# RG-LRU steps paced one by one behind the chunks of a two-layer hybrid block, with state sums in PSUM

## The chip, the cores and the metric

The kernel runs on one core of a Trainium2 chip. The metric is the device time of one execution in microseconds (us). The time before is the median of three runs.

The engines are named as in the profile: PE (TensorE, matmuls; PEld is its weight load), DVE (VectorE), ACT (ScalarE), POOL (GpSimd) and SP (the queue that issues most DMAs). SBUF is the on-chip memory, PSUM the memory that matmuls write.

## The reference, cut to what matters

Two layers, each over 512 tokens of width 1024. One input projection feeds three branches, and their gated outputs go through one output projection.

```python
for l in range(DEPTH):
    xn = rms_norm(h, ln_g[l])
    proj = xn @ w_in[l]
    u_a, z_a, u_b, z_b, q_lat, kv_lat, k_rope, z_c = jnp.split(proj, pts, axis=-1)
    y_a = rwkv7_mix(u_a, ...)           # a recurrence over tokens, 8 heads of 64x64 state
    y_b = rms_norm(rglru_mix(u_b, ...), lru_out_g[l])
    y_c = rms_norm(mla_mix(q_lat, kv_lat, k_rope, ...), mla_out_g[l])
    y = concatenate([y_a * silu(z_a), y_b * silu(z_b), y_c * silu(z_c)])
    h = h + y @ w_out[l]
return rms_norm(h, final_g)

def rglru_mix(u, ...):                  # the RG-LRU branch
    xc = conv_b + sum(up[:, j:j + T] * conv_w[j] for j in range(4))
    gate_r = sigmoid(xb @ ga_w + ga_b); gate_i = sigmoid(xb @ gx_w + gx_b)
    log_a = -8 * gate_r * softplus(-lam)
    a = exp(log_a)
    bx = sqrt(-expm1(2 * log_a)) * (gate_i * xc)
    h = scan over tokens of  h = a * h + bx
```

## The kernel before, in words

Tokens lie along the columns, channels on the 128 partitions. A projection (`proj`) is 24 matmuls of 512 columns: 8 slices of the input, each with three products (lines 233 to 235), since every float32 operand is split into a rounded high part H and the remainder L. For a weight tile, `weights` loads the raw tile `wr`, rounds it on ACT to `wH`, and subtracts on POOL or DVE to `wL` (line 229); a counter with the modulus `wmod` sends every `wmod`-th of these subtractions to DVE. The high and low parts of activations are made by `ysplit` (ACT, then line 211 on DVE).

The RWKV recurrence is done in 8 chunks of 64 tokens, one after the other (`chunk`, step `H`). Chunk `ch` corrects its values from the state (PE line 849, then two additions on DVE, line 852), makes its contribution to the state (PE line 859), adds the old state (DVE line 863) and multiplies by the decay (DVE line 864; chunk 0 has only line 866) into a new state tile `S`. Every second chunk also makes the outputs of two chunks (PE lines 877 and 883, copied by DVE line 885 and squared by ACT line 886, reduced by DVE line 887). So the chunks are a serial chain that goes PE, DVE, PE, DVE, DVE, PE. Other work has to fill the engines meanwhile.

That other work is, in this stage: the RG-LRU branch's four tiles of 128 channels. `lru_a(j)` (step `A`) projects tile `j`, does the convolution (three DVE operations, line 681), makes two gates on PE (line 687) with their sigmoids, the product of gate and input (POOL line 691) and a tanh. `lru_b` (step `B`, two tiles per call) makes the decay and the factor: exp on ACT, a square on POOL (line 702), two DVE operations (704 and 705), a square root on ACT, a product on POOL (710), then the scan on DVE (712), its square for the norm (ACT lines 716 and 718, POOL line 719) and the gated product on DVE (720). Then there are the group norm of the recurrence (`N`), the latent products of the attention branch (`t`, 8 slices of 12 matmuls with 416 columns), the gates of that branch (`g`, one projection each), its latent statistics (`T1`) and the sums over tokens of the RG-LRU's squares (`R`, PE line 379).

The order in which this is written is the string `ORD3`, one letter and a number per step. A scheduler then places the instructions on each engine's queue, by the order of writing and by its own estimate of when inputs are ready. Each queue runs strictly in order. `act` chains those ACT operations that need a function table, and loads a table when the set changes.

Of the kernel before, what the change touches and what calls it, by code (L numbers as in the profile page):

```python
# [11 lines left out]
AF = mybir.ActivationFunctionType  # L12
# [35 lines left out]
def body(ctx, tc, x, wc, wl, wo, w2a2, gagx, wuq, wukv, vec, ln_g, fin_g, cst, out, depth=DEPTH):  # L48
# [17 lines left out]
    WA, WB, WC, WD = 1000, 2, 2, 5  # L66
# [5 lines left out]
    def g2(shape=(128, 512)):  # L72
        return tl("g2", shape, F32, bufs=11)
# [132 lines left out]
    def f(ap):  # L206
        return ap.bitcast(F32)
# [113 lines left out]
    def one_layer(l):  # L321
# [350 lines left out]
        def lru_a(*js, o=None):  # L672
            for j in js:
                o = o or proj(17 + j)
                ub = g2([128, T + 3])
                G.memset(ub[:, 0:3], 0.0)
                copy(ub[:, 3:], o)
                xc = g2()
                A.activation(out=xc, in_=o, func=AF.Identity, scale=vc("cw", 12 + j), bias=vc("cb", j))
                for t in range(3):  # L680
                    V.scalar_tensor_tensor(out=xc, in0=ub[:, t:t + T], scalar=vc("cw", 4 * t + j), in1=xc, op0=ALU.mult, op1=ALU.add)  # L681
                gt = []
                for w in range(2):
                    o = ps()
                    for e in range(2):
                        hr = slice(64 * e, 64 * e + 64)
                        PE.matmul(o[hr, :], gw[hr, w, j, :], xc[hr, :], start=True, stop=True)  # L687
                    s = g2()
                    act(s, o, AF.Sigmoid, bias=vc("gx_b" if w else "ga_b", j))
                    gt.append(s)  # L690
                G.tensor_tensor(out=gt[1], in0=gt[1], in1=xc, op=ALU.mult)
                th = g2()
                act(th, gt[0], AF.Tanh, scale=sp8[:, l, j:j + 1])
                st[j] = (gt[0], gt[1], th)
                o = None

        def lru_b(*js):
            for j in js:
                a, bx, th = st[j]
                act(a, a, AF.Exp, scale=nsp8[:, l, j:j + 1])  # L700
                a2 = g2()
                G.tensor_tensor(out=a2, in0=a, in1=a, op=ALU.mult)

                V.scalar_tensor_tensor(out=a2, in0=a2, scalar=1.0, in1=th, op0=ALU.add, op1=ALU.mult)
                V.tensor_scalar(out=a2, in0=a2, scalar1=1.0e-34, scalar2=None, op0=ALU.max)  # L705
                st[j] += (a2,)
            for j in js:
                a, bx, th, a2 = st[j]
                act(a2, a2, AF.Sqrt)
                G.tensor_tensor(out=bx, in0=bx, in1=a2, op=ALU.mult)  # L710
                hs = th
                V.tensor_tensor_scan(out=hs, data0=a, data1=bx, initial=0.0, op0=ALU.mult, op1=ALU.add)
                sq = a2
                if j == 0:
                    stb[0] = tl("sqn", [128, T])
                    A.activation(out=stb[0], in_=hs, func=AF.Square)
                else:
                    A.activation(out=sq, in_=hs, func=AF.Square)
                    G.tensor_tensor(out=stb[0], in0=stb[0], in1=sq, op=ALU.add)
                V.scalar_tensor_tensor(out=hs, in0=hs, scalar=vc("out_g", j), in1=gz[j], op0=ALU.mult, op1=ALU.mult)  # L720
                yb.append(hs)

# [118 lines left out]
        def chunk(ch):  # L841
            cp, par = ch // 2, ch % 2
            ur = slice(64 * (1 - par), 64 * (1 - par) + 64)
            if ch:
                uo = [ck([128, 4, 64]) for _ in range(2)]
                for p in range(4):
                    for e in range(2):
                        hr = slice(64 * e, 64 * e + 64)
                        PE.matmul(uo[e][ur, p, :], AR[p][hr, 0, ch * 64:(ch + 1) * 64], S[ch][hr, p, :], start=True, stop=True)
                for e in range(2):  # L850
                    u = UV[ur, :, ch, 64 * e:64 * e + 64]
                    V.tensor_tensor(out=u, in0=uo[e][ur, :, :], in1=u, op=ALU.add)
            if ch < 7:
                so = ck([128, 4, 64])
                for p in range(4):
                    for e in range(2):
                        hr = slice(64 * e, 64 * e + 64)
                        hc = slice(e * 64, (e + 1) * 64)
                        PE.matmul(so[hr, p, :], BT[p][:, ch, hc], UV[:, p, ch, hc], start=True, stop=True)
                sn = S[ch + 1] = tl("S", [128, 4, 64], bufs=3)  # L860
                pc = PC[:, :, ch:ch + 1].to_broadcast([128, 4, 64])
                if ch:
                    V.tensor_tensor(out=sn, in0=so, in1=S[ch], op=ALU.add)
                    V.tensor_tensor(out=sn, in0=sn, in1=pc, op=ALU.mult)
                else:
                    V.tensor_tensor(out=sn, in0=so, in1=pc, op=ALU.mult)
# [34 lines left out]
        def lat_products(kk):  # L901
            wmod[0] = WC
# [42 lines left out]
        steps.update({"H": chunk, "N": lambda _: group_norm(), "A": lru_a, "B": lambda i: lru_b(2 * i, 2 * i + 1), "R": b_sums, "Y": b_split,  # L945
# [280 lines left out]
```

## Time and profile before

| what | value |
|---|---|
| median of 3 runs | 852.93 us (851.06 to 854.30) |
| the profiled execution's own time | 854.13 us |
| its span, first to last instruction | 852.3 us |
| mean granted clock of PE | 0.986 |
| PE busy | 793.0 us, 93% |
| DVE, ACT, POOL busy | 561.1, 518.6, 326.3 us |
| ACT table loads | 31, of 1283 ns each in the mean |
| DMA | 91.07 MB, mean 107 GB/s |

The profile has one page of sums over the whole execution, and views of the trace that can be cut to a window. In a timeline row the columns are start, duration, engine, line, operation, output<-inputs, the shape, the count, and in brackets the idle time ahead of it with what ended it. In a row of waits they are the total, how many, and the longest. Line numbers of the profile are those of the kernel before; the changed kernel's lines are some 5 to 31 higher.

### The profile page before, as it was taken

What the parts mean: (1) busy time and instruction counts of PE and PEld (TensorE: products, weight loads), DVE (VectorE), ACT (ScalarE), POOL (GpSimd) and SP (SyncE); (2) the same over time, 40 slices, a digit from 0 to 9 for tenths busy, and PEclk for the clock granted to TensorE, in tenths of its full rate; (3) what the DMA queues carried; (4) which work ended last, traced back from release to release, by engine and by line L of the source; (5) the groups of instructions that cost most, each with busy time, mean ns of one, the idle gap of its engine ahead of it and who ended that gap; (6) DMA issues with size and microseconds to landing.
All of it is one profiled execution on the core that took longest, in us unless ns stands there. A gap on an engine that the chain in (4) does not pass through costs nothing.

```text
span 852.3 us, 15212 instructions
## 1 busy us (share of the span) xinstructions
PE 793.0 (93%) x5696; PEld 619.7 (73%) x5696; DVE 561.1 (66%) x1145; ACT 518.6 (61%) x1018; POOL 326.3 (38%) x299
## 2 busy tenths in 40 slices
PE   3999999999879999999979999999997899899995
PEld 3878888886659867656778788888765697675674
DVE  5578776924976486774474976695367955677636
ACT  5667876557563666564367677845566436665634
POOL 0455557522462332012344556574143524210223
PEclk9999999999998999999999999999999899999998
DMA  7322233311113365123733233232001235631354
GB/s 235 106 75 65 72 112 128 114 59 31 32 48 103 131 215 185 52 86 101 266 116 99 75 99 99 100 111 94 27 26 42 81 100 156 235 102 50 111 173 161
DMA packets 49754, 91.07 MB, mean 107 GB/s; under 512 B 5520, under 2 KB 8336, under 8 KB 49680
## 3 DMA queue, kind: packets, MB, share of 16 engines
q1 hardware_dynamic: 49104, 89.05, 32.5%
q8 instruction: 45, 0.74, 0.4%
q10 hardware_dynamic: 576, 1.05, 0.3%
q14 instruction: 29, 0.24, 0.1%
HBM read 73.30 MB, written 16.78 MB: 106 GB/s over the span
## 4 chain that ended last, share of the span: by engine, by line
PE 65%; DVE 15%; ACT 10%; DMA 4%; issue 3%; POOL 3%; SPq 0%; ACTq 0%; DVEq 0%; POOLq 0%
PE acc L233 15%; PE acc L234 14%; PE acc L235 14%; PE acc L1058 4%; PE ck L1084 3%; ACT g L138 3%; PE ps L1076 2%; ACT wH L141 1%; ACT UV L141 1%; PE ps L687 1%; DMA hp<-dr 1%; DVE g L681 1%; PE ps L611 1%; ACT L136 1%; PE ps L629 1%
## 5 line engine op out<-in xcount | busy, mean ns | idle before, releaser
L229 POOL TENSOR_TENSOR wL<-wr,wH 128x512 fp32r<-128x512 f32 (+1 forms) x126 | 170.4, 1355 | 298.2 <-ACT wH L141 270.7
L141 ACT ACTIVATE wH<-wr 128x512 fp32r<-128x512 f32 (+1 forms) x192 | 118.7, 621 | 139.9 <-PE acc L234 74.5
L233 PE MATMUL acc<-xH,wH 128*128 128x512 f32 (+1 forms) x496 | 192.6, 389 | 0.0
L234 PE MATMUL acc<-xL,wH 128*128 128x512 f32 (+1 forms) x496 | 189.8, 383 | 0.4 <-DVE xL L306 0.2
L235 PE MATMUL acc<-xH,wL 128*128 128x512 f32 (+1 forms) x496 | 189.1, 382 | 0.0
L233 PEld LDWEIGHTS acc<-xH,wH 128*128 128x128 f32 x496 | 94.4, 191 | 18.2 <-ACT xH L141 0.7
L235 PEld LDWEIGHTS acc<-xH,wL 128*128 128x128 f32 x496 | 94.5, 190 | 17.2
L234 PEld LDWEIGHTS acc<-xL,wH 128*128 128x128 f32 x496 | 94.5, 190 | 16.9 <-DVE xL L306 0.9
L229 DVE TENSOR_TENSOR wL<-wr,wH 128x512 fp32r<-128x512 f32 (+1 forms) x66 | 50.9, 774 | 72.2 <-ACT wH L141 72.2
L233 PE MATMUL acc<-wH,c 128*128 128x512 f32 x192 | 81.9, 427 | 1.4 <-DVE hp L428 1.1
L234 PE MATMUL acc<-wL,c 128*128 128x512 f32 x192 | 76.3, 397 | 0.0
L235 PE MATMUL acc<-wH,c 128*128 128x512 f32 x192 | 76.1, 397 | 0.0
L141 ACT ACTIVATE UV<-ps 64x512 f32<-64x512 f32 (+4 forms) x112 | 52.3, 494 | 30.5 <-PE ps L1076 22.4
L233 PEld LDWEIGHTS acc<-wH,c 128*128 128x128 f32 x192 | 36.1, 188 | 12.0 <-DVE hp L428 2.0
L138 ACT ACTIVATE c<-acc,sm 128x128 f32<-128x128 f32 (+3 forms) x64 | 33.6, 526 | 18.3 <-DVE sm L1060 18.1
L1058 PE MATMUL acc<-am,am 128*128 128x128 f32 (+3 forms) x128 | 42.3, 447 | 0.9 <-ACT c L138 0.8
L234 PEld LDWEIGHTS acc<-wL,c 128*128 128x128 f32 x192 | 36.2, 189 | 8.4 <-issue 1.4
L235 PEld LDWEIGHTS acc<-wH,c 128*128 128x128 f32 x192 | 36.1, 188 | 8.2 <-issue 0.5
L369 POOL TENSOR_TENSOR g<-g,g 128x512 f32<-128x512 f32 x24 | 32.2, 1340 | 24.1 <-ACT g L138 24.1
L136 ACT ACT_TABLE_LOAD x31 | 39.8, 1283 | 1.3 <-PEq L1214 0.7
L138 ACT ACTIVATE g<-g 128x512 f32<-128x512 f32 (+1 forms) x58 | 36.4, 628 | 4.6 <-DVE g L705 2.6
L141 ACT ACTIVATE c<-g 128x512 fp32r<-128x512 f32 (+1 forms) x40 | 24.9, 628 | 17.0 <-DVE g L720 7.0
(219 smaller groups left out, 1590.8 us busy)
## 6 DMA issues: line engine op xcount, KB each, us to landing
wr<-in_wc_dram SPq DMA_DIRECT2D x116, 256.0 KB, 2.6
wr<-in_wo_dram SPq DMA_DIRECT2D x48, 256.0 KB, 3.4
hp<-dr SPq DMA_DIRECT2D x38, 256.0 KB, 3.5
dr<-hp SPq DMA_DIRECT2D x28, 256.0 KB, 2.9
dr<-g SPq DMA_DIRECT2D x16, 256.0 KB, 2.6
g<-dr SPq DMA_DIRECT2D x16, 256.0 KB, 3.4
wr<-in_wl_dram SPq DMA_DIRECT2D x16, 208.0 KB, 2.5
dr<-c SPq DMA_DIRECT2D x12, 256.0 KB, 3.8
```

The lines of the kernel that those rows point to most:

```text
L136: chained(A.preload_act_table_set(SETS[st]))
L138: chained(A.activation(out=out, in_=in_, func=func, **kw))
L141: i = A.activation(out=out, in_=in_, func=AF.Copy, **kw)
L229: (V if wn[0] % wmod[0] == 0 or wn[0] <= 4 else G).tensor_tensor(out=L, in0=raw, in1=f(H), op=ALU.subtract)
L233: PE.matmul(o, a[0], b[0], start=start, stop=False)
L234: PE.matmul(o, a[0], b[1], start=False, stop=False)
L235: PE.matmul(o, a[1], b[0], start=False, stop=stop)
L369: G.tensor_tensor(out=z, in0=z, in1=s, op=ALU.mult)
L611: PE.matmul(os[e][:, cp, :].rearrange("p (x s) -> p x s", x=2), bk[rr, ch, :, :].rearrange("p x s -> p (x s)"), ar[rr, :, ch * 64:(ch + 1) ...
L1058: PE.matmul(o[:, 0:n], qT[:, hd, qt * 128:n], K2[:, p, e, 0:n], start=True, stop=True)
L1076: PE.transpose(o[:, (qt - kt) * 128:(qt - kt + 1) * 128], Pm[p][e, qt][:, kt * 128:(kt + 1) * 128], ident)
L1084: i = PE.matmul(ot[e * 64:(e + 1) * 64, k2 * 128:T], Vt[:, k2, 2 * p + e, :], PT[:, 2 * (k2 % 2) + e, 0:(4 - k2) * 128], start=(k2 == 0), ...
```

## The change

The change does five things, the same in both layers.

1. The RG-LRU steps are cut into single operations. `conv_steps(j)` projects tile `j` and gives back its three convolution operations as a list; `lru_b_steps` gives back, for each tile, a factor, a scan and a gated product. `A` and the new step `b` put them on the list `paced`. At two places of each chunk, behind the second correction and behind the state product, `pace` takes the next one from the list and issues it behind that DVE instruction (`tc.issue_after`: what the block issues on that instruction's engine comes after it on the queue; how long after is left to the scheduler).
2. The gates of tiles 2 and 3 are steps of their own (`a2`, `a3`), whose PE products come behind the last state product written so far (chunk 5's and chunk 6's in the order of the string).
3. The second half of the branch (tiles 2 and 3: factors, scans, gated products) comes behind chunk 7's last correction (`B1`), with its operations issued plainly.
4. The square of the decay goes from POOL to ACT. The state's sum is written in place in PSUM, so that the product behind it reads PSUM.
5. `ORD3` is new: the latent products `t` follow the group norm at once, the attention gates `g` come behind them, and `T1` stands ahead of `g2` and `g3`. While chunks are written, and for the latent slices 0 and 6, weight subtractions all go to POOL (`WE = 1000`). Counted over the whole program, 66 subtractions on DVE and 126 on POOL become 60 and 132.

```diff
-    ORD3 = "B0 H0 H1 A2 H2 H3 A3 H4 H5 H6 H7 B1 N0 g0 g1 t0 t6 t1 t2 t4 t5 t3 t7 T0 R0 Y0 g2 g3 T1"
+    ORD3 = "b0 H0 H1 A2 H2 A3 H3 H4 H5 a2 H6 H7 a3 B1 N0 t0 t6 t1 t2 t4 t5 t3 t7 T0 R0 g0 Y0 g1 T1 g2 g3"
...
+        paced, mark = [], {}
+        def pace(ins):
+            if paced:
+                with tc.issue_after(getattr(ins, "ins", ins)):
+                    paced.pop(0)()
...
-                G.tensor_tensor(out=a2, in0=a, in1=a, op=ALU.mult)
+                A.activation(out=a2, in_=a, func=AF.Square)
...
+            return [lambda f=f, j=j: f(j) for j in js for f in (factor, scan, gated)]
+        def lru_b_behind(_):
+            with tc.issue_after(mark["V"]):
+                for s in lru_b_steps(2, 3):
+                    s()
+        def gates_behind(j):
+            with tc.issue_after(mark["P"]):
+                lru_gates(j)
...
         def chunk(ch):
+            wmod[0] = WE
...
-                    V.tensor_tensor(out=u, in0=uo[e][ur, :, :], in1=u, op=ALU.add)
+                    i = V.tensor_tensor(out=u, in0=uo[e][ur, :, :], in1=u, op=ALU.add)
+                mark["V"] = i.ins
+                pace(i)
...
                 if ch:
-                    V.tensor_tensor(out=sn, in0=so, in1=S[ch], op=ALU.add)
-                    V.tensor_tensor(out=sn, in0=sn, in1=pc, op=ALU.mult)
-                else:
-                    V.tensor_tensor(out=sn, in0=so, in1=pc, op=ALU.mult)
+                    V.tensor_tensor(out=so, in0=so, in1=S[ch], op=ALU.add)
+                pace(V.tensor_tensor(out=sn, in0=so, in1=pc, op=ALU.mult))
...
-            wmod[0] = WC
+            wmod[0] = WE if kk in (0, 6) else WC
...
+        steps.update({"H": chunk, "N": lambda _: group_norm(), "A": lambda j: paced.extend(conv_steps(j)), "a": gates_behind,
+                      "b": lambda _: paced.extend(lru_b_steps(0, 1)), "B": lru_b_behind, "R": b_sums, "Y": b_split,
                       "t": lat_products, "T": latents, "g": lambda p: gzc.append(gate(25 + p))})
```

The orders that follow are of layer 0; layer 1 has the same. DVE between the corrections of chunk 2 and of chunk 3, before (`UV` rows are the corrections, `S` rows the state, `wL` a weight subtraction, `c_513` and `c_514` low parts of finished RG-LRU tiles, 681 the convolution):

```order
L852 TENSOR_TENSOR UV_319<-ck,UV_319 64x4x64 x2
L229 TENSOR_TENSOR wL_2719<-wr_2716,wH_2718 128x512
L229 TENSOR_TENSOR wL_2762<-wr_2759,wH_2761 128x512
L211 TENSOR_TENSOR c_513_2959<-g_386_1997,c_513_2959 128x512
L211 TENSOR_TENSOR c_514_2962<-g_398_2140,c_514_2962 128x512
L863 TENSOR_TENSOR S_2377<-ck,S_2264 128x256
L864 TENSOR_TENSOR S_2377<-S_2377,PC_320 128x256
L681 SCALAR_TENSOR_TENSOR g_438_2482<-g_437_2479,vecs,g_438_2482 128x512 x2
L852 TENSOR_TENSOR UV_319<-ck,UV_319 64x4x64 x2
```

And now (882 is the correction, 896 and 897 the state, 719 and 720 the factor, 727 the scan):

```order
L882 TENSOR_TENSOR UV_319<-ck,UV_319 64x4x64
L719 SCALAR_TENSOR_TENSOR g_418_2342<-g_418_2342,g_398_2140 128x512
L896 TENSOR_TENSOR ck<-ck,S_2253 128x256
L720 TENSOR_SCALAR g_418_2342<-g_418_2342 128x512
L897 TENSOR_TENSOR S_2356<-ck,PC_320 128x256
L211 TENSOR_TENSOR c_504_2917<-g_386_1997,c_504_2917 128x512
L727 SCALAR_TENSOR_TENSOR g_398_2140<-g_395_2132,g_397_2137 128x512
L229 TENSOR_TENSOR wL_2760<-wr_2757,wH_2759 128x416
L882 TENSOR_TENSOR UV_319<-ck,UV_319 64x4x64 x2
```

The weight subtractions and convolution steps have left this place; the second tile's factor and scan stand here, with one subtraction for the latent weights behind the scan.

DVE around chunk 7 and the second scans, before (712 is the scan, 720 the gated product):

```order
L852 TENSOR_TENSOR UV_319<-ck,UV_319 64x4x64
L712 SCALAR_TENSOR_TENSOR g_423_2357<-g_420_2348,g_422_2354 128x512
L712 SCALAR_TENSOR_TENSOR g_443_2498<-g_440_2490,g_442_2495 128x512
L863 TENSOR_TENSOR S_2601<-ck,S_2539 128x256
L229 TENSOR_TENSOR wL_2809<-wr_2806,wH_2808 128x416
L864 TENSOR_TENSOR S_2601<-S_2601,PC_320 128x256
L720 SCALAR_TENSOR_TENSOR g_423_2357<-g_423_2357,vecs,g_352_1723 128x512
L720 SCALAR_TENSOR_TENSOR g_443_2498<-g_443_2498,vecs,g_367_1818 128x512
L852 TENSOR_TENSOR UV_319<-ck,UV_319 64x4x64 x2
```

And now, behind chunk 7 and the group norm (its last scaling is line 926):

```order
L926 TENSOR_TENSOR c_446_2601<-c_446_2601,vr_457_2680 128x512
L719 SCALAR_TENSOR_TENSOR g_455_2658<-g_455_2658,g_444_2567 128x512
L720 TENSOR_SCALAR g_455_2658<-g_455_2658 128x512
L719 SCALAR_TENSOR_TENSOR g_456_2669<-g_456_2669,g_454_2653 128x512
L727 SCALAR_TENSOR_TENSOR g_444_2567<-g_441_2558,g_443_2564 128x512
L720 TENSOR_SCALAR g_456_2669<-g_456_2669 128x512
L229 TENSOR_TENSOR wL_2832<-wr_2829,wH_2831 128x416
L737 SCALAR_TENSOR_TENSOR g_444_2567<-g_444_2567,vecs,g_352_1723 128x512
L229 TENSOR_TENSOR wL_2896<-wr_2893,wH_2895 128x512
L727 SCALAR_TENSOR_TENSOR g_454_2653<-g_451_2645,g_453_2650 128x512
```

The two scans stood between chunk 6's correction and its state; they now stand behind the group norm, and the subtraction for the last latent slice (`wL_2832`) stands behind the first of them.

PE at the end of the latent products, before (`sqn` holds the RG-LRU's squares, summed on POOL behind the last scan):

```order
L235 MATMUL acc_2785<-wH_2916,xL_105 128x416
L379 MATMUL ck<-ones_96,sqn_2227 128x2 x4
L233 MATMUL acc_2971<-xH_104,wH_2974 128x512
L234 MATMUL acc_2971<-xL_105,wH_2974 128x512
L235 MATMUL acc_2971<-xH_104,wL_2975 128x512
```

And now:

```order
L234 MATMUL acc_2700<-wL_2832,xH_104 128x416
L235 MATMUL acc_2700<-wH_2831,xL_105 128x416
L1011 MATMUL ps_3130<-C,c_405_2257 128x128
L1011 MATMUL ps_3130<-C,c_430_2427 128x128
L233 MATMUL acc_2874<-xH_104,wH_2877 128x512
L234 MATMUL acc_2874<-xL_105,wH_2877 128x512
L235 MATMUL acc_2874<-xH_104,wL_2878 128x512
L233 MATMUL acc_2874<-xH_104,wH_2877 128x512
L234 MATMUL acc_2874<-xL_105,wH_2877 128x512
L379 MATMUL ck<-ones_96,sqn_2243 128x2 x4
```

The sums over tokens stay close behind the latent products, 2 transposes and 5 products later, while the scans that they need have moved from ahead of chunk 7 to behind the group norm.

More of the change, by code (lines that the diff above doesn't have):

```diff
@@ L670, in one_layer @@
         st = {}
-        def lru_a(*js, o=None):
-            for j in js:
[L674 to L695, printed above, removed]
@@ L697, in lru_b, with conv_steps @@
-        def lru_b(*js):
-            for j in js:
+        paced, mark = [], {}
[3 more added lines that the diff above has]
+                    paced.pop(0)()
+        def conv_steps(j, o=None):
+            o = o or proj(17 + j)
+            ub = g2([128, T + 3])
+            G.memset(ub[:, 0:3], 0.0)
+            copy(ub[:, 3:], o)
+            xc = st[j] = g2()
+            A.activation(out=xc, in_=o, func=AF.Identity, scale=vc("cw", 12 + j), bias=vc("cb", j))
+            return [lambda t=t: V.scalar_tensor_tensor(out=xc, in0=ub[:, t:t + T], scalar=vc("cw", 4 * t + j), in1=xc, op0=ALU.mult, op1=ALU.add)
+                    for t in range(3)]
@@ new lines, in lru_gates @@
+        def lru_gates(j):
+            xc, gt = st[j], []
+            for w in range(2):
+                o = ps()
+                for e in range(2):
+                    hr = slice(64 * e, 64 * e + 64)
+                    PE.matmul(o[hr, :], gw[hr, w, j, :], xc[hr, :], start=True, stop=True)
+                s = g2()
+                act(s, o, AF.Sigmoid, bias=vc("gx_b" if w else "ga_b", j))
+                gt.append(s)
+            G.tensor_tensor(out=gt[1], in0=gt[1], in1=xc, op=ALU.mult)
+            th = g2()
+            act(th, gt[0], AF.Tanh, scale=sp8[:, l, j:j + 1])
+            st[j] = (gt[0], gt[1], th)
@@ L699, in lru_b, with lru_a, lru_b_steps, factor @@
+        def lru_a(j, o=None):
+            for s in conv_steps(j, o):
+                s()
+            lru_gates(j)
+        def lru_b_steps(*js):
+            for j in js:
+                a = st[j][0]
+                act(a, a, AF.Exp, scale=nsp8[:, l, j:j + 1])
+            def factor(j):
                 a, bx, th = st[j]
-                act(a, a, AF.Exp, scale=nsp8[:, l, j:j + 1])
                 a2 = g2()
-                G.tensor_tensor(out=a2, in0=a, in1=a, op=ALU.mult)
+                A.activation(out=a2, in_=a, func=AF.Square)
@@ L714, in lru_b, with scan @@
+            def scan(j):
+                a, bx, th, sq = st[j]
+                V.tensor_tensor_scan(out=th, data0=a, data1=bx, initial=0.0, op0=ALU.mult, op1=ALU.add)
                 if j == 0:
                     stb[0] = tl("sqn", [128, T])
-                    A.activation(out=stb[0], in_=hs, func=AF.Square)
+                    A.activation(out=stb[0], in_=th, func=AF.Square)
                 else:
-                    A.activation(out=sq, in_=hs, func=AF.Square)
+                    A.activation(out=sq, in_=th, func=AF.Square)
```

16 lines of the change are left out of this document (7 added, 9 removed).

## The prediction, made before the changed kernel was run

> **What bounds the kernel now.** I read the busy shares first, then the chain that ended last, then TensorE's waits in the stage that the change touches, then the granted clock there.
>
> ```profile
> PE 793.0 (93%) x5696; PEld 619.7 (73%) x5696; DVE 561.1 (66%) x1145; ACT 518.6 (61%) x1018; POOL 326.3 (38%) x299
> PE 65%; DVE 15%; ACT 10%; DMA 4%; issue 3%; POOL 3%; SPq 0%; ACTq 0%; DVEq 0%; POOLq 0%
> ```
>
> TensorE (PE) is busy for 93% of the span and carries most of the chain. The change removes no matmul, so time can only come from PE's idle stretches and from stretches at a lowered clock. The stage of the chunks (layer 0: 205 to 262 us, layer 1 the same 416 us later) has both:
>
> ```profile
> 205.00:262.00 57.00, 47.61 (x629) 35.46 (x626) 44.78 (x71) 34.75 (x55) 26.29 (x21) 0.94 0.18 52
> 262.00:300.00 38.00, 38.00 (x191) 34.52 (x190) 20.04 (x67) 17.30 (x40) 13.93 (x11) 1.00 0.34 114
> 621.00:678.00 57.00, 47.54 (x629) 35.10 (x626) 44.10 (x69) 34.25 (x54) 26.27 (x21) 0.94 0.16 47
> ...
> PE ck L849 <- DVE S L864: 4.6, 3, 3.1
> PE ps L883 <- DVE UV L852: 2.6, 4, 1.6
> PE ps L687 <- DVE g L681: 2.1, 1, 2.1
> ```
>
> The columns of the first three are the length, then PE, weight load, VectorE (DVE), ScalarE (ACT) and GpSimd (POOL) busy, then the clock. PE is idle for 57.0 - 47.6 = 9.4 us per layer, and the three waits of layer 0 add up to 9.3: all are for DVE. In the 38 us behind, PE never idles. The clock falls behind the longest wait, and not behind one of 2.13:
>
> ```profile
> 225.60 1.93 PE L687 MATMUL ps<-g,w 64*64 64x512 f32 x8 [2.13 <-DVE g L681]
> 254.83 0.51 PE L849 MATMUL ck<-S,c 64*64 64x64 f32 x10 [3.11 <-DVE S L864]
> ...
> 220.00:230.00 10.00, 7.87 (x49) 5.08 (x47) 9.87 (x14) 6.45 (x12) 4.61 (x4) 1.00 0.22 65
> 256.00:258.00 2.00, 1.39 (x24) 1.08 (x18) 2.00 (x5) 1.26 (x2) 0.00 (x0) 0.50 0.96 327
> 258.00:260.00 2.00, 2.00 (x28) 1.79 (x27) 1.74 (x4) 0.38 (x1) 0.00 (x0) 0.50 0.25 95
> 260.00:262.00 2.00, 2.00 (x7) 1.76 (x6) 0.76 (x2) 1.31 (x3) 0.00 (x0) 0.50 0.00 0
> ```
>
> Half of the busy time between 256 and 262 (1.39 + 2.00 + 2.00 = 5.4 us) is lost: 2.7 us. Waits and clock cost 12 us per layer, 24 in all, which is the most that the change could win in this stage.
>
> **Why DVE is late.** In the wait of 3.11 us DVE runs two scans, a weight split and two state operations in line:
>
> ```profile
> 248.45 3.42 DVE L712 TENSOR_TENSOR_SCAN g<-g,g 128x512 f32<-128x512 f32 x2
> 252.24 1.14 DVE L229 TENSOR_TENSOR wL<-wr,wH 128x416 fp32r<-128x416 f32 x1
> 253.30 1.48 DVE L864 TENSOR_TENSOR S<-S,PC 128x256 f32<-128x256 f32 x1
> ...
> 250.75 3.75 POOL L719 TENSOR_TENSOR sqn<-sqn,g 128x512 f32<-128x512 f32 x2
> ...
> L864 DVE TENSOR_TENSOR S<-S,PC 128x256 f32<-128x256 f32 x6 | 4.8, 800 | 0.1
> L866 DVE TENSOR_TENSOR S<-ck,PC 128x256 f32<-128x256 f32 x1 | 0.4, 423 | 1.0 <-PE ck L859 1.0
> L739 DVE TENSOR_TENSOR ck<-ck,xt 128x240 f32<-128x240 f32 x2 | 0.8, 416 | 0.1
> ```
>
> L864 and L866 have one size, yet the one whose two inputs lie in SBUF takes 0.80 us in the mean, and 1.48 beside a POOL operation; the one that reads PSUM takes 0.42.
>
> **State sums in PSUM.** The new sum works in place in PSUM, as L739 does (0.416 us for 240 columns), and its product then reads PSUM like L866. That is 6 x 0.38 = 2.3 us per layer off the chain of the states (bounds 0 and 2.3). How much reaches PE is counted in the walk below.
>
> **The walk through the new order.** I walk PE and DVE through the listed order of the changed kernel with the durations of these rows, 0.07 us for a handover between other engines (212.56 to 212.64 below) and an estimated 0.25 for one to PE:
>
> ```profile
> 210.68 0.69 DVE L704 SCALAR_TENSOR_TENSOR g<-g,g 128x512 f32<-128x512 f32 x1 [0.94 <-POOL g L702]
> 211.41 0.43 DVE L705 TENSOR_SCALAR g<-g 128x512 f32<-128x512 f32 x1
> 211.93 0.63 ACT L138 ACTIVATE g<-g 128x512 f32<-128x512 f32 x1
> 212.64 1.28 POOL L710 TENSOR_TENSOR g<-g,g 128x512 f32<-128x512 f32 x1 [1.99 <-ACT g L138]
> 213.95 1.22 DVE L712 TENSOR_TENSOR_SCAN g<-g,g 128x512 f32<-128x512 f32 x1 [0.22 <-POOL g L710]
> 221.22 0.64 ACT L718 ACTIVATE g<-g 128x512 f32<-128x512 f32 x1 [1.12 <-DVE g L712]
> 242.45 0.54 ACT L141 ACTIVATE wH<-wr 128x416 fp32r<-128x416 f32 x1
> 261.24 0.59 DVE L229 TENSOR_TENSOR wL<-wr,wH 128x416 fp32r<-128x416 f32 x1 [1.31 <-ACT wH L141]
> 234.23 1.07 POOL L229 TENSOR_TENSOR wL<-wr,wH 128x416 fp32r<-128x416 f32 x1 [4.29 <-DVE S L864]
> 237.15 0.77 DVE L852 TENSOR_TENSOR UV<-ck,UV 64x256 f32<-64x256 f32 x2 [1.46 <-PE ck L849]
> 238.17 0.69 PE L859 MATMUL ck<-UV,c 128*64 128x64 f32 x16
> 235.01 0.69 DVE L887 TENSOR_REDUCE vr<-c 128x8 f32<-128x512 f32 x1 [0.45 <-ACT c L886]
> 280.62 0.40 PE L234 MATMUL acc<-xL,wH 128*128 128x512 f32 x1
> ...
> 291.07 0.39 PE L235 MATMUL acc<-xH,wL 128*128 128x512 f32 x1
> 276.10 0.35 PE L233 MATMUL acc<-wH,xH 128*128 128x416 f32 x1
> ...
> 279.31 0.35 PE L235 MATMUL acc<-wH,xL 128*128 128x416 f32 x1
> ```
>
> A 512-column product takes (291.07 - 280.62) / 46 = 0.23 us, a 416-column one (279.31 - 276.10) / 17 = 0.19.
>
> *Gates' products later:* the wait of 2.13 us (L687) goes: line 681's operations now lie singly in chunks 4 to 6, and the products stand behind chunk 6's state product. I take it as won in full (bounds 0 and 2.13); what is late next are the corrections of chunks 2 and 3, since each factor, scan and gated product paced behind a chunk's operation stands ahead of the next chunk's on DVE, and PE's products for that chunk wait with it.
>
> *Chunks 0 and 1:* about 0.5 us of waits, as now.
>
> *Chunk 2:* from chunk 1's corrected values on, in line: factor 0.69 + 0.43, square root 0.63, a POOL split 1.07 ahead of POOL's product 1.28, scan 1.22, reduction 0.69, half a correction 0.38, gated product 0.7, the other half 0.38; with 0.5 of handovers 8.0 us. PE meanwhile has chunk 1's 64-column work (2.4) and 18 products (4.1), with the changes between kinds 7.0. Wait 1.0 (0 to 2.5).
>
> *Chunk 3:* the second scan stands ahead of the correction, and a weight split behind the scan, whose rounded weights wait on ACT behind the scan's square: state sum 0.42, maximum 0.43, root 0.63, product 1.28, scan 1.22, square 0.64, rounding 0.54, split 0.59, correction 0.77, handovers 0.8: 7.3 us. PE has 16 products (3.7), the state's products 0.7 and some 0.4 of small ones: 4.8. Wait 2.5 at least; with one POOL split (1.07) ahead of its product 3.5, which I take; with two operations held up by POOL ones 5.0. This is above the 3.11 that lowered the clock, so the 2.7 us stay.
>
> *Chunks 4 to 7:* single convolution steps, hidden by PE's fill. Handovers alone leave an estimated 0.15 and 0.6 in turn, where only 64-column work stands between: 1.5 (0.5 to 3.0).
>
> *Second scans later:* here a cover goes. The low half of the last latent weight now stands on DVE behind the group norm, two factors and scan 2:
>
> ```profile
> 262.47 0.18 DVE L892 TENSOR_SCALAR vr<-vr 128x32 f32<-128x32 f32 x1
> ...
> 267.03 2.50 DVE L895 TENSOR_TENSOR c<-c,vr 128x512 f32<-128x512 f32 x4
> ```
>
> From chunk 7's first finished half: copies, squares and reduction 2.0, small operations 4.6 (262.47 to 267.03), scalings 2.5, factor 1.1, root 0.7, POOL's product 1.35, scan 1.3, maximum 0.4, split 0.6, handover 0.25: 14.8 us. PE has the other half 0.5, the gates' products 1.9, 51 latent products 9.7 and 0.5 of changes: 12.6. Wait 2.2 (1.0 to 3.5). Then the sums over tokens (L379) wait for scan 3: factor and root, two POOL operations, scan, square and POOL's last sum end 6 us behind that split, and PE has 10 latent products, 2 transposes and 5 products, 3.5 us. I take 2.2 (0.5 to 3.5). Today this place has no wait.
>
> *Six weight splits go from DVE to POOL, eight squares from POOL to ACT.* They lie inside the walk. SP issues the same loads in the new order of weights; I cost that at nothing, covered by the rounded weights that stand ready; uncovered, each would add its wait to PE's.
>
> *Latent statistics ahead of gates 2 and 3:* DVE is then freer where PE waits for `hp`, and I take 0.5 of this row (0 to 0.74):
>
> ```profile
> 305.33 0.50 PE L233 MATMUL acc<-wH,c 128*128 128x512 f32 x1 [0.74 <-DVE hp L428]
> ```
>
> **Sum.** Waits 0.5 + 1.0 + 3.5 + 1.5 + 2.2 + 2.2 = 10.9 against 9.3: +1.6; later -0.5; clock 0. That is +1.1 per layer, +2.2 in all: 856.3 on the profiled execution's own 854.13 us, and 855.1 on the median of 852.93 shown, which is 1.2 below it. I say 855.0.
>
> [...] By the rows, L864 took 1.48 us beside POOL's 3.75 for two. [...]
>
> **Rivals.** *Faster:* chunk 3's POOL split is early, its wait stays near 2, so that the clock holds as behind 2.13, and PE's small work covers most of the late waits. For it: each wait is a small difference of long sums. Against it: the listed order. Per layer clock -2.7, chunk 3 -1.2, late -2.0: 855.1 - 11.8 = 843.3. *Slower:* DVE's scan chains wait for whole POOL operations, as L864 did. In chunk 3 1.5 more; at the last split 1.3 more, which makes that wait 3.5 us. It decides from one held operation in each chain on: +2.8 per layer, 860.7; where 3.5 us lowers the clock a second time, +2.7 more, 866.1. I take 863.4. *The pacing doesn't do what it says:* "behind a chunk's own" can also mean ahead of the next chunk's, as the listed order shows in chunks 2 and 3; this is inside the forecast.
>
> **How the numbers follow.** Forecast 0.44, faster rival 0.33, slower rival 0.23. A measurement here can tell about 0.5% (4.3 us) from no change, so no change is 848.7 to 857.2. The forecast's own range is 849 to 860; of its chance 0.31 lies within 0.5% and 0.13 above. So faster 0.33, same 0.31, slower 0.36. The range goes from just below the faster rival to just above the slower one, 841 to 866, and leaves out about 2 in 10, the sums with most bounds at one end.
>
> **What would show it.** Right: PE waits of over 2 us for chunk 3's corrections, about 2 us for the last split and for the sums, none for the gates, and the new state product at 0.42. Wrong: no lowered clock in the stage (faster rival), or two stretches of it (slower); a state sum in PSUM above 0.5 us; PE waits at a place that this walk has covered.

## The result, and the profile after

The changed kernel takes 874.47 us (median of 4 runs, 872.44 to 874.79), the kernel before 852.76 beside it. The ratio is 1.025, 95% interval 1.023 to 1.027: it is 2.5% slower, 21.7 us, and lies outside the predicted range. The profiled run took 872.44 us with a span of 870.7 us and a mean granted clock of 0.975 (before: 852.3 and 0.986).

First the page of the changed kernel: the busy line, and the engines' shares of the chain that ended last.

```profile
PE 800.9 (92%) x5696; PEld 624.6 (72%) x5696; DVE 561.4 (64%) x1139; ACT 520.4 (60%) x1026; POOL 320.6 (37%) x297
PE 65%; DVE 14%; ACT 9%; issue 5%; DMA 3%; POOL 3%; SPq 1%; ACTq 0%; DVEq 0%; POOLq 0%
```

As many matmuls as before, 7.9 us more of busy time (at the lowered clock they are longer: behind 327.38 a 512-column product takes 0.63 us, at full speed 0.39), and 10.5 us more idle. On the chain "issue" went from 3% to 5% and SP's queue (SPq) from 0% to 1%: a first hint that an order, not an engine's work, is late.

The milestones of layer 0 say where. These are PE's first out-projection product and its first score product, the first two rows of before, the others of the changed kernel (its lines are up to 33 higher, and L1090 is L1058 of before):

```profile
291.65 0.47 PE L233 MATMUL acc<-wH,c 128*128 128x512 f32 x1
336.88 1.65 PE L1058 MATMUL acc<-am,am 128*128 128x128 f32 x8
```

```profile
293.63 0.48 PE L233 MATMUL acc<-wH,c 128*128 128x512 f32 x1
346.40 1.64 PE L1090 MATMUL acc<-am,am 128*128 128x128 f32 x8
```

Until the out-projection the change loses 2.0 us, near the 1.6 that the walk through the chunks and the latent products gave, though not for its reasons, as shown below. From there to the scores, a stage that the prediction credited with 0.5 us won, it loses 7.5 us more. By the first scores of layer 1 (754.42 and 772.98 us) it has lost 18.6 us: the same again. This stretch, from the first out-projection product to the first score product, is the measure for the experiments: 45.2 us before (layer 1: 46.2), 52.8 changed (53.4), 14.8 us more in the two layers of the 18.4 by which the spans differ.

The stage of the chunks and the 38 us behind it, by window (length, then PE, weight load, VectorE, ScalarE, GpSimd busy, clock, DMA share, GB/s), and PE's waits over the whole program (sum, number, longest):

```profile
205.00:262.00 57.00, 51.98 (x662) 41.76 (x658) 39.76 (x78) 31.09 (x52) 15.33 (x15) 0.94 0.15 44
262.00:300.00 38.00, 33.88 (x143) 27.65 (x143) 25.43 (x60) 23.95 (x55) 18.42 (x14) 0.91 0.31 99
```

```profile
PE acc L233 <- DVE hp L428: 11.3, 4, 5.1
PE ck L891 <- DVE UV L882: 9.9, 6, 3.9
PE acc L234 <- DVE wL L229: 7.1, 3, 3.2
PE ck L379 <- POOL sqn L733: 3.2, 2, 3.0
```

In the chunks PE is idle for 5.0 us instead of 9.4. The waits for states and gates of before are gone from this window; those for corrected values (L882) have come. In the 38 us behind, PE is idle for 4.1 us, where it never was before, and the mean clock is 0.91 instead of 1.00. So PE idles about as long as before in the two windows together (9.1 us), and the loss until the out-projection comes from the clock. The first row is the surprise: four waits for `hp`, the partial sums of the out-projection, add up to 11.3 us (4.5 before). The waits of layer 0 one by one:

```profile
227.52 1.12 PE L891 MATMUL ck<-UV,c 128*64 128x64 f32 x16 [3.89 <-DVE UV L882]
...
265.25 0.71 PE L234 MATMUL acc<-wL,xH 128*128 128x416 f32 x1 [3.23 <-DVE wL L229]
...
307.55 0.47 PE L233 MATMUL acc<-wH,c 128*128 128x512 f32 x1 [0.91 <-DVE hp L428]
310.75 0.66 PE L994 MATMUL ps<-C,g 128*128 128x128 f32 x4 [1.35 <-DVE c L998]
327.38 0.77 PE L233 MATMUL acc<-c,wH 128*128 128x512 f32 x1 [4.45 <-DVE hp L428]
```

The last one is the first key product. It needs an accumulator which the adds of line 428 give back, and stands where PE waited 0.96 us before. Behind three of these waits (3.89, 3.23 and 4.45 us) the clock falls. Behind the first it is 0.50 from 228 to 232; behind the last two:

```profile
266.00:268.00 2.00, 2.00 (x7) 1.89 (x7) 2.00 (x2) 1.38 (x2) 2.00 (x2) 0.50 0.45 131
268.00:270.00 2.00, 2.00 (x8) 1.75 (x7) 2.00 (x5) 0.19 (x1) 0.09 (x1) 0.50 0.11 20
...
328.00:330.00 2.00, 2.00 (x6) 1.60 (x5) 1.81 (x3) 0.95 (x2) 0.00 (x0) 0.50 0.50 134
330.00:332.00 2.00, 2.00 (x6) 1.53 (x5) 0.00 (x0) 1.23 (x3) 0.00 (x0) 0.50 1.04 391
```

**Followed back from 327.38.** On VectorE the adds of line 428 stand behind the last bonus steps, whose products on GpSimd (L1008) are late because their loads are. SP's queue of the changed kernel (its rows give the time at which a transfer was issued):

```profile
305.43 0.33 SPq L1007 DMA_DIRECT2D g<-dr  x1
305.99 0.33 SPq L221 DMA_DIRECT2D wr<-in_wukv_dram  x1
306.77 0.33 SPq L1006 DMA_DIRECT2D g<-dr  x1
311.19 0.33 SPq L221 DMA_DIRECT2D wr<-in_wukv_dram  x1
311.62 1.41 SPq L430 DMA_DIRECT2D dr<-hp  x3
313.12 0.51 SPq L430 DMA_DIRECT2D dr<-c  x1
314.89 0.33 SPq L421 DMA_DIRECT2D hp<-in_x_dram  x1
315.32 0.40 SPq L1007 DMA_DIRECT2D g<-dr  x1
```

and the same place of before, where the second load from `wukv` stands behind all of these, the last bonus loads and two `hp` loads lying between its two rows:

```profile
308.34 0.32 SPq L975 DMA_DIRECT2D g<-dr  x1
...
310.88 0.42 SPq L221 DMA_DIRECT2D wr<-in_wukv_dram  x1
```

That load brings the value weights (`WW["v"]`). In the changed kernel SP reaches it at 307.1 and issues nothing until 311.19: its buffer (`wr`, three of them) is still being read on GpSimd.

```profile
308.19 1.30 POOL L1008 TENSOR_TENSOR g<-g,g 128x512 f32<-128x512 f32 x1 [4.34 <-DVE hp L428]
309.44 1.72 POOL L229 TENSOR_TENSOR wL<-wr,wH 128x512 fp32r<-128x512 f32 x1
313.96 1.28 POOL L229 TENSOR_TENSOR wL<-wr,wH 128x512 fp32r<-128x512 f32 x1 [2.80 <-ACT wH L141]
319.59 2.58 POOL L1008 TENSOR_TENSOR g<-g,g 128x512 f32<-128x512 f32 x2 [4.35 <-issue]
```

The subtraction ends at 309.44 + 1.72 = 311.16, and the load goes out 0.03 us later, with the stores and the bonus loads behind it. The next bonus gate is issued at 315.32 instead of 308.34: 7 us later, 5 of them lost since the out-projection began. GpSimd's two products start at 319.59, and PE's wait ends at 327.38.

### The profile page after: what moved, and what is told of

Read it like the earlier page. It is cut to its first block, busy times and chain, and to the rows that moved or that the text cites. A ratio compares the mean times of both kernels' runs of the same rounds, so it can differ in the third digit from the quotient of the medians.

```text
span 870.7 us, 15203 instructions
## 1 busy us (share of the span) xinstructions
PE 800.9 (92%) x5696; PEld 624.6 (72%) x5696; DVE 561.4 (64%) x1139; ACT 520.4 (60%) x1026; POOL 320.6 (37%) x297
## 4 chain that ended last, share of the span: by engine, by line
PE 65%; DVE 14%; ACT 9%; issue 5%; DMA 3%; POOL 3%; SPq 1%; ACTq 0%; DVEq 0%; POOLq 0%
PE acc L233 15%; PE acc L234 14%; PE acc L235 14%; PE acc L1090 4%; PE ck L1116 3%; PE ps L1108 2%; ACT g L138 2%; ACT wH L141 1%; PE ps L695 1%; ACT UV L141 1%; PE ps L611 1%; DVE g L727 1%; POOL g L722 1%; PE ps L629 1%; PE ps L815 1%
## 5 line engine op out<-in xcount | busy, mean ns | idle before, releaser
L229 POOL TENSOR_TENSOR wL<-wr,wH 128x512 fp32r<-128x512 f32 (+1 forms) x132 | 178.1, 1352 | 318.0 <-ACT wH L141 316.8
L234 PE MATMUL acc<-xL,wH 128*128 128x512 f32 (+1 forms) x496 | 189.7, 383 | 0.4 <-DVE xL L306 0.2
L234 PEld LDWEIGHTS acc<-xL,wH 128*128 128x128 f32 x496 | 95.0, 191 | 17.2 <-DVE xL L306 0.9
L234 PE MATMUL acc<-wL,c 128*128 128x512 f32 x192 | 76.3, 398 | 0.7 <-DVE wL L229 0.6
L1090 PE MATMUL acc<-am,am 128*128 128x128 f32 (+3 forms) x128 | 42.3, 447 | 0.9 <-ACT c L138 0.8
L234 PEld LDWEIGHTS acc<-wL,c 128*128 128x128 f32 x192 | 36.2, 189 | 9.1 <-DVE wL L229 1.5
```

The source lines that it names most:

```text
L229: (V if wn[0] % wmod[0] == 0 or wn[0] <= 4 else G).tensor_tensor(out=L, in0=raw, in1=f(H), op=ALU.subtract)
L234: PE.matmul(o, a[0], b[1], start=False, stop=False)
L1090: PE.matmul(o[:, 0:n], qT[:, hd, qt * 128:n], K2[:, p, e, 0:n], start=True, stop=True)
```

## The experiments

**Theory Q**: the load of the value weights, moved ahead in SP's queue, holds up what stands behind it. **Theory T**: the order of the latent statistics, now ahead of gates 2 and 3, costs the time. **Theory S**: the second scans and the gates' products come later, and all behind them with them. Ratios are to the kernel before, run beside each.

**e1: only the load moved back.**

```diff
-                WW["v"] = weights(wukv[l, :, 512:1024])
+                with tc.issue_after(misc["ya"]):   # the last bonus load
+                    raw = tl("wr", [128, 512], F32, bufs=3)
+                    nc.sync.dma_start(out=raw, in_=wukv[l, :, 512:1024])
+                WW["v"] = weights(None, raw=raw)
```

> The changed kernel with one DMA moved: the load of the value weights stands behind the last load of the bonus steps in SP's queue, as in the kernel before; nothing else of the order is touched. Theory Q (the load, moved ahead, holds up SP's queue while it waits for a free buffer): the 4.45 us wait for DVE's hp near 327 us falls to about 1 us in each layer and the third lowered clock goes with it, 2 x (3.4 + 2.5) = 12 us less: 860 to 865 us. Theory T (VectorE's own order at the end of the stage, the latent statistics put ahead of two gates): the wait stays, 872 to 876. Theory S (the second scans and the gates' products come later, everything behind is 2 us late and the wait follows from that): no more than 3 us less, 871 to 875.

Measured 864.40 us, ratio 1.0124 (1.0106 to 1.0142): 10 us come back through one DMA's place. The key product's wait, in e1:

```profile
325.48 0.47 PE L233 MATMUL acc<-c,wH 128*128 128x512 f32 x1 [2.61 <-DVE hp L428]
```

It fell from 4.45 to 2.61, not to 1, and in layer 1 from 5.10 to 1.57. The lowered clock behind it is gone in layer 1 alone; in layer 0 it fell here too (0.51 between 326 and 328). The stretch is 49.9 and 47.4 us. Q is right in the sum, and something else still holds this place.

**e2: the old order behind the group norm**, pacing and PSUM sums kept. (The subtractions for gates 0 and 1 now follow the chunks with `WE` still in force, so they all go to GpSimd: VectorE has 56 in the whole program instead of 60.)

```diff
-    ... a3 B1 N0 t0 t6 t1 t2 t4 t5 t3 t7 T0 R0 g0 Y0 g1 T1 g2 g3
+    ... a3 B1 N0 g0 g1 t0 t6 t1 t2 t4 t5 t3 t7 T0 R0 Y0 g2 g3 T1
```

> The changed kernel with the old order behind the group norm (gates 0 and 1 ahead of the latent products, the statistics last); the pacing in the chunks and the sums in PSUM stay. Theory Q: the load stands at its old place in SP's queue by this too, and the two gates' 16 us of products cover the second scans, so the waits of 3.23 and 4.45 us and both clock drops behind them go: what is left is the chunk stage, whose waits are about 3 us per layer shorter than before: 846 to 853 us. Theory T: the same, since the statistics are last again. Theory S (later second scans): the loss stays, over 862.

Measured 855.25 us, ratio 1.0021 (1.0008 to 1.0034): the large loss is gone, but the kernel is not faster than before, which theories Q and T expected (846 to 853 us). A wait stands there that none of the theories had; first PE's row, then ScalarE's rows in e2:

```profile
267.60 0.72 PE L233 MATMUL acc<-wH,xH 128*128 128x416 f32 x1 [4.56 <-ACT g L141]
```

```profile
266.44 0.63 ACT L732 ACTIVATE g<-g 128x512 f32<-128x512 f32 x1 [2.91 <-DVE g L727]
266.97 0.58 ACT L141 ACTIVATE g<-acc 128x512 f32<-128x512 f32 x1
```

ScalarE stands at the square of scan 3 (L732), which waits for the scan on VectorE (L727). The copy of gate 1 out of its accumulator is queued behind it, and the latent products, which use all four accumulators, wait for that copy. So a part of S holds: scans that run late hold ScalarE in line. e8 tests it.

**e3: only the statistics last** (`g1 T1 g2 g3` becomes `g1 g2 g3 T1`). The load goes back to its old place in SP's queue with it.

> The changed kernel with only the latent statistics put back behind the four gates; the gates' products stay behind the latent products. In the listed order the load of the value weights goes back to its old place in SP's queue with it. Theory Q and theory T both expect the 4.45 us wait and the third clock drop gone, while the 3.23 us wait for the last latent weight and its clock drop stay: 860 to 865 us. Theory S: 871 to 875. With the first run it tells Q from T: Q wants both to fall alike, T only this one.

Measured 857.74 us, ratio 1.0047 (1.0024 to 1.0070), 6.7 us below e1 and better than expected of either theory. T is right too: with the load at its old place in both, the order of the statistics costs 6.7 us. In e3 the stretch behind the chunks is 45.2 and 45.7 us, as before the change: nothing of the large loss is left.

**e4: the kernel before with the new order behind the group norm.**

> The kernel before with only the new order behind the group norm; its scans stay ahead of it, in the old places, and the state sums in SBUF. The load of the value weights stands ahead in SP's queue as in the changed kernel. Theory Q: the wait near 327 us and the lowered clock come here too, +12 us, and the last latent weight waits little, since the scans are done: 860 to 867 us. Theory S (the later scans are the cause): 850 to 856. Theory T: as Q.

Measured 868.19 us, ratio 1.0177 (1.0152 to 1.0203): just above the range of Q. The new order alone costs 14.6 us, without pacing, PSUM sums or later scans. The key product's wait is longer than in the changed kernel, the stretch 54.1 and 53.7 us (16.4 us above before in all), and SP again issues nothing from 302.9 until the subtraction on GpSimd ends (307.03):

```profile
325.31 0.76 PE L233 MATMUL acc<-c,wH 128*128 128x512 f32 x1 [6.51 <-ACT c L141]
```

```profile
307.05 0.33 SPq L221 DMA_DIRECT2D wr<-in_wukv_dram  x1
```

The releaser named is ScalarE, but its copy (324.53 to 325.16) and the first add of line 428 (324.42 to 325.16) end together, and both follow the last bonus steps on VectorE.

**e5: the kernel before with only the load moved ahead** (the first four stores of line 430 are ordered behind it).

```diff
+                for d in held:          # the stores of the first half
+                    tc.add_manual_dep(d, i.ins.name, NOSYNC, reason="issue order")
```

> The kernel before, with nothing but the load of the value weights put ahead of the first stores of the partial sums in SP's queue, the place that it has in the changed kernel. Theory Q (the load at the head of SP's queue waits for a buffer and holds up the stores and the bonus loads behind it): PE's wait for hp near 320 us grows from about 1 to 4 us or more and the clock falls behind it, +4 to +6.5 per layer: 861 to 867 us. Theory T (the order of the statistics and the gates costs the time, the load only goes with it): 852 to 856.

Measured 857.12 us, ratio 1.0046 (1.0028 to 1.0063). The load costs here too, 5.3 us, above T's range and below Q's. SP hardly waits for the buffer in this kernel (0.8 us; the load goes out at 304.55, the stores at 304.94), and measured from the out-projection the first of the last three bonus loads is issued only 0.2 us later than before. But the three then take 5.4 to 6.0 us from issue to landing, where before they took 3.4 to 4.4.

So here the early load costs by a later landing of what stands behind it, and not by a held issue; why these transfers take longer was not shown. GpSimd's last two bonus products start 2.2 us later from the out-projection on, the key product waits 3.36 us instead of 0.96, and the stretch is 49.2 and 48.5 us.

**e9: e3 with the load moved ahead**, the fourth corner.

> The kernel of e3 (statistics last) with the load of the value weights put ahead of the first stores in SP's queue, as in the changed kernel; with the changed kernel, e1 and e3 the fourth corner of load early or late by statistics early or late. If the early load costs what it cost the kernel before (e5: 5.3 us), whatever the order of the statistics: 863 us (861 to 865). If it costs what it cost the changed kernel (e1: 10 us): 868 (866 to 870). If the load only hurts together with the early statistics: 857 to 859.

Measured 862.56 us, ratio 1.0130 (1.0102 to 1.0158), within the range of the first case. The four corners, medians in us (ratios; the stretch of both layers together, 91.4 us before the change):

| | load early | load late |
|---|---|---|
| statistics ahead of gates 2, 3 | 874.47 (1.0251; 106.2), the changed kernel | 864.40 (1.0124; 97.3), e1 |
| statistics last | 862.56 (1.0130; 95.7), e9 | 857.74 (1.0047; 90.9), e3 |

The load costs 10.1 us in the upper row and 4.8 in the lower one (8.9 and 4.8 by the stretch). By the medians alone that difference is unsure, since e9's interval is as wide. The stretches of the single layers speak for it: the load costs 2.9 us in layer 0 and 6.1 in layer 1 in the upper row, 0.8 and 4.1 in the lower one, some 2 us more in each. (Layer 1 of e9 pays more because the clock falls there behind the key product's wait, of 3.19 us, and not in layer 0 behind one of 2.14: the products that follow take 0.63 us there, and 0.40 in layer 0.) Why the load should cost more in the upper row is read on GpSimd and was not tried apart. In e9 the subtraction that frees the buffer stands ahead of the bonus product; in the changed kernel it stood behind it (308.19, 309.44 above). GpSimd and SP of e9:

```profile
306.40 1.29 POOL L229 TENSOR_TENSOR wL<-wr,wH 128x512 fp32r<-128x512 f32 x1 [4.11 <-issue]
307.66 1.27 POOL L1012 TENSOR_TENSOR g<-g,g 128x512 f32<-128x512 f32 x1
```

```profile
307.72 0.33 SPq L1049 DMA_DIRECT2D wr<-in_wukv_dram  x1
```

The load goes out right behind the subtraction again (306.40 + 1.29 = 307.69), at 307.72 instead of 311.19. SP issues nothing for 3.0 us ahead of it (from 304.71), instead of 4.1.

**e6: the kernel before with the state sums in PSUM alone.**

> The kernel before with only the state sums in PSUM. As the prediction has it the chain of the states is up to 2.3 us per layer shorter; the 3.11 us wait for a state (whose sum took 1.48 us in SBUF) falls to about 2.0, and if so the clock does not fall behind it: 843 to 850 us. If the chain is covered elsewhere, so that PE waits for the scans on VectorE whatever the sum takes: 852 to 855.

Measured 851.60 us, ratio 0.9991 (0.9977 to 1.0004): no change that stands clear of the noise. PE's rows in e6 show why:

```profile
252.07 0.51 PE L849 MATMUL ck<-S,c 64*64 64x64 f32 x10 [2.05 <-DVE S L864]
255.41 1.97 PE L883 MATMUL ps<-UV,am 128*64 128x64 f32 x30 [1.80 <-DVE UV L852]
```

The wait for the state fell from 3.11 to 2.05 as worked out, but the next wait, for chunk 7's values, grew from 0.61 to 1.80, so that the two together are no shorter (3.85 against 3.72). The clock fell there all the same (0.50 from 254 to 258), which the expectation had not.

**e11: e8 (below) with the sums back in SBUF.**

> The kernel of e8 with the state sums back in SBUF. By the prediction's term the chain of the states is 2.3 us per layer longer: 847 to 850 us. As e6 had it in the kernel before, what the sums give is given back at the next wait: 842 to 846.

Measured 846.66 us, ratio 0.9937 (0.9919 to 0.9955), against 844.09 for e8. By the medians the sums in PSUM are worth 2.6 us in the paced chunks, 1.3 per layer, between the two expectations; by the ratios 3.5 us. The two intervals just touch, and the ten runs of e11 spread from 844.2 to 850.7, so this is at the edge of the noise.

**e7: every latent weight's low half on GpSimd**, on e3 (`wmod[0] = WE` for all). The edit does more than that: the modulus stays at 1000 behind the latent products until the next step that sets it. Of VectorE's 60 subtractions 44 go to GpSimd, and only 6 of these are for latent weights.

> The kernel of e3 (statistics last) with every latent weight's low half worked out on GpSimd, so that none stands behind the second scans on VectorE. If the 3.1 us wait and the clock drop behind it are what is left of the loss: 2 x (3.1 + 2) = 10 us less than e3's 857.7, 845 to 851 us. Rival: GpSimd, which also has two products of each scan and the gates' products, is now late with the splits, and the wait only changes its releaser: 855 to 860.

Measured 865.42 us, ratio 1.0154 (1.0127 to 1.0180): worse than e3, and than the rival's range. GpSimd in e7:

```profile
257.00 5.09 POOL L229 TENSOR_TENSOR wL<-wr,wH 128x416 fp32r<-128x416 f32 x3
262.05 1.71 POOL L733 TENSOR_TENSOR sqn<-sqn,g 128x512 f32<-128x512 f32 x1
263.73 1.28 POOL L722 TENSOR_TENSOR g<-g,g 128x512 f32<-128x512 f32 x1
```

Three subtractions, 5.09 us, now stand between the products of scans 2 and 3, so scan 3 starts 13.7 us behind the start of the group norm's last scalings instead of 12.6. The 3.1 us wait for VectorE is gone, and waits of 1.23, 2.40 and 2.96 us for GpSimd and ScalarE have taken its place. Against that, chunk 3's wait fell from 3.86 to 1.41 us, and the clock held there (the 16 products behind the wait took 0.69 us instead of 1.12). By the out-projection e7 is level with e3 (293.04 and 293.13 us). Some of the loss stands in other stages, behind subtractions that only moved along; this wait and one of 2.82 us at 843.8 have no counterpart in e3:

```profile
422.24 0.79 PE L234 MATMUL acc<-wL,c 128*128 128x512 f32 x1 [3.02 <-POOL wL L229]
```

So e7 does not price the latent subtractions alone.

**e8: e2 with the second scans issued behind gates 0 and 1** instead of right behind the last correction.

```diff
-            with tc.issue_after(mark["V"]):
-                for s in lru_b_steps(2, 3):
-                    s()
+            for s in lru_b_steps(2, 3):
+                s()
-    ... a3 B1 N0 g0 g1 t0 ...
+    ... a3 N0 g0 g1 B1 t0 ...
```

> The kernel of e2 (old order behind the group norm) with the second scans issued behind the first two gates instead of right behind the last correction. In e2 PE waits 1.4 and 4.6 us for ScalarE to copy the gates out of PSUM, since ScalarE stands at the squares of scans 2 and 3; if that is all, both waits and the clock drop go, 2 x (6 + 2) = 16 us less than 855.3: 838 to 846 us. Rival: the scans, now beside the latent products, hold up VectorE's splits of the latent weights or the token sums behind them, and PE waits there instead: 849 to 857.

Measured 844.09 us, ratio 0.9896 (0.9868 to 0.9924): 11.2 us below e2, and 7.7 us faster than the kernel before, its whole computation kept. The two waits for the gates' copies are gone. Behind the chunks, up to the out-projection, one long wait remains in e8, with a short fall of the clock behind it (0.62 and 0.53 from 276 to 280):

```profile
274.74 0.49 PE L379 MATMUL ck<-ones,sqn 128*128 128x2 f32 x3 [2.23 <-POOL sqn L733]
```

**e10: e8 with the token sums and the splits of the scans' outputs behind gate 2** (`T0 g2 R0 Y0 g3 T1`).

> The kernel of e8 with the token sums and the weight splits of the scans' outputs issued behind gate 2 instead of ahead of it. In e8 PE waits 2.2 us in each layer for GpSimd's last sum of squares and its clock falls behind it; gate 2's 8 us of products should cover that: 2 x (2.2 + 0.8) = 6 us less than 844.1: 836 to 841 us. Rival: the scans' outputs are now split too late for the first out-projection, behind only one gate, and the wait stands there: 843 to 850.

Measured 843.54 us, ratio 0.9893 (0.9864 to 0.9921): the same as e8, and within the rival's range, though the wait stands elsewhere than the rival had it: gate 2's first product waits 2.63 us (2.69 in layer 1) for ScalarE's copy of an accumulator.

**e12: e8 with the factors of scans 2 and 3 back behind the last correction.**

> The kernel of e8 with the factors of scans 2 and 3 (two VectorE operations, roots and one GpSimd product each) back behind the last correction; only the scans, their squares and gated products stay behind the first two gates. If the 2.2 us wait for the token sums in e8 follows from the length of the chain behind gate 1, it and the lowered clock go, 2 x (2.2 + 0.8): 837 to 841 us. Rival: the roots on ScalarE again stand ahead of the copies of the gates, and PE waits for a free accumulator as in e2, 1.4 us or more in each layer: 842 to 848.

Measured 858.31 us, ratio 1.0075 (1.0045 to 1.0104): the rival's mechanism, but far dearer. PE waits 1.35 and 1.22 us for the gates' copies, 1.32 for a rounded weight and 2.97 for a subtraction on GpSimd, within 15 us in each layer.

## Why the prediction was wrong

- **The walk through the chunks found the right waits.** Chunk 2 waited 0.69 us (predicted 1.0), chunk 3 3.89 (3.5), chunks 4 to 7 0.39 (1.5), the last latent weight 3.23 (2.2), the token sums 0.22 and, in layer 1, 2.98 (2.2). A wait of 0.80 for an earlier tile's gates, ahead of the chunks, stood in no term; the handover to PE, an estimate of 0.25 us for which it named no row, took 0.05 behind the last latent split (265.20 to 265.25). With that gate layer 0 waits 9.2 us, where the sum had 10.9. That the walk's +1.6 per layer met the trace's +2.0 is luck: PE waits no longer than before (9.3), and a fall of the clock that the sum left out makes the difference. e3, where the two faults below are absent, is 4.2 us slower than before in all.
- **Chunk 3's wait comes from the new order behind the group norm**, and not from pacing alone. The subtraction that stands behind the second scan is for a latent weight that this order brings forward:

```profile
225.48 1.32 DVE L229 TENSOR_TENSOR wL<-wr,wH 128x416 fp32r<-128x416 f32 x1 [1.13 <-ACT wH L141]
```

In e2 the gates' weights stand there instead, with their subtractions on GpSimd; chunk 3 then waits 1.65 us, in e7 1.41, and in both the clock holds (the 16 products behind the wait take 0.69 us, in the changed kernel 1.12).

- **The clock was mis-sized.** The forecast kept one fall per layer. In layer 0 a second one follows the 3.23 us wait: about half of 2.00 + 2.00 + 1.78 us of busy time between 266 and 272, 2.9 us. That is the second half of the slower rival (2.7 us), for which it asked 3.5 us. In layer 1 the clock holds behind the same wait (3.22 us; 1.00 from 690 to 694) and falls behind the next, the 2.98 us for the token sums (0.54 from 698 to 700).
- **The step that failed** is "SP issues the same loads in the new order of weights; I cost that at nothing, covered by the rounded weights that stand ready". It asked whether PE would want for weights, and no wait of PE ends with a load of them (its 7.1 us of waits for low halves, L234 above, end with VectorE's queue). It did not ask what is queued behind a load whose buffer is not free. One load that had stood behind the stores and the last bonus loads now stood ahead of them and waited for its buffer; moving it back gives 10.1 us (e1). Waiting for the buffer need not be the whole price: in e5 the load cost 5.3 us with hardly a wait, as the transfers behind it landed later.
- **The sign of a term failed with it**: "Latent statistics ahead of gates 2 and 3 [...] I take 0.5". With the load at its old place their order costs 6.7 us (e1 against e3). It puts gate 3 right ahead of the out-projection; in the traces the out-projection starts at 293.61 in e1 and 293.13 in e3, but GpSimd's first bonus product at 302.46 and 300.66, and the adds of line 428 at 306.57 and 304.09. In e1 PE also waits 0.68 us for a gate's copy within the out-projection (296.64), and not in e3. That the gate is what delays them was read from the traces and not tried apart.
- **PSUM sums**: new sums and products take 0.43 and 0.42 us as predicted. Their 2.3 us per layer were an upper bound: no clear gain in the kernel before (e6), some 1.3 in paced chunks (e11). The mean of 0.80 us that they were worked out from mixes two kinds. Before, the six products of layer 0 (L864) took 0.42, 0.95, 0.42, 0.43, 1.11 and 1.48 us; the three long ones ran beside a GpSimd operation and the short ones did not, with both inputs in SBUF like the others:

```profile
216.65 0.42 DVE L864 TENSOR_TENSOR S<-S,PC 128x256 f32<-128x256 f32 x1
```

The products that read PSUM took 0.41 to 0.43 us beside GpSimd operations too. So what the change gains on these products is what GpSimd did to them.

- **The rivals.** All lay in the stage of the chunks and of the latent products, so the range ended at 866. The slower rival had one row to go by, L864's: 253.30 + 1.48 = 254.78, 0.28 us behind the end of GpSimd's two sums (250.75 + 3.75 = 254.50). What it expected from it, that operations on VectorE wait for GpSimd's to end, does show there, once in each of its two chains: the subtraction in chunk 3 took 1.32 us beside GpSimd's sum of squares (225.09 to 226.35) instead of 0.58, and the first late scan 2.28 beside a subtraction (261.75 to 263.30), where the second, alone, took 1.21:

```profile
262.10 2.28 DVE L727 TENSOR_TENSOR_SCAN g<-g,g 128x512 f32<-128x512 f32 x1
268.56 1.21 DVE L727 TENSOR_TENSOR_SCAN g<-g,g 128x512 f32<-128x512 f32 x1
```

The subtraction ended 0.45 us behind GpSimd's operation and the scan 1.08, so all three ended behind it by their time alone (0.42, 0.58 and 1.21 us) less 0.13 or 0.14. These two make 1.8 us per layer (1.32 - 0.58 and 2.28 - 1.21) of the 2.8 that the rival gave, which the forecast had not counted. They play no visible part in the large loss behind the out-projection.

Of the 21.7 us, then, the places of one load and of the statistics make 16.7 (the changed kernel against e3). The other 5 lie ahead of the out-projection, where the second fall of the clock is the largest new item. Open is why the scheduler puts that load where it does when the statistics move.

## What to carry to other kernels

Here a change of order on the compute engines also changed the order of the DMA queue. List that queue for before and after, and for each transfer that moved ahead ask when its buffer comes free, and what stands behind it: the price was that of the transfers behind it, which were issued later (the changed kernel, 10.1 us by e1) or landed later (e5, 5.3 us), not of its own.

Where two engines work in line, moving late work off one put it ahead of something on the other (e2, e7, e12: PE then waited 4.56, 2.96 and 2.97 us in layer 0). The fastest versions (e8, 844.09 us, and e10, 843.54) moved the late scans behind the copies that free accumulators, so that these copies no longer stood queued behind the scans' waits.

## What the runs showed of the hardware that was not expected

The prediction took a wait of over 3 us as what lowers the clock, as in the rows of before. The runs bear out no such bound, from either side. In layer 0 of the changed kernel a wait of 3.23 us lowered it; in layer 1 the same wait (3.22, ending at 689.55) left it at full speed for the next 7 us. In e10 a wait of 2.63 us left it there in layer 0 (the products behind it took 0.39 us), and one of 2.69 at the same place in layer 1 lowered it (0.63 us). In e11 it fell 1.1 us behind a wait of only 1.68 us (ending at 226.13), ahead of any further wait; in e8 the same wait (1.64, ending at 226.71) left it at full speed. First the changed kernel, then two rows of e11, then e8, by window, with the clock third from the right:

```profile
691.00:693.00 2.00, 2.00 (x11) 1.49 (x9) 2.00 (x3) 0.68 (x2) 1.38 (x1) 1.00 0.26 96
```

```profile
227.00:227.25 0.25, 0.25 (x10) 0.25 (x10) 0.25 (x1) 0.25 (x2) 0.25 (x1) 0.95 0.00 0
227.25:227.50 0.25, 0.25 (x12) 0.25 (x9) 0.25 (x1) 0.25 (x1) 0.25 (x2) 0.50 0.27 66
```

```profile
228.00:230.00 2.00, 1.30 (x42) 1.13 (x37) 1.97 (x4) 0.98 (x2) 1.70 (x2) 1.00 0.00 0
```

So one and the same wait gave either result, and what decides between them no run here shows. In a kernel like this one a wait from about 1.7 us on (1.68 in e11) is best counted as a possible fall of the clock, not a certain one.
